# A list scheduler that models a port shared by VectorE and GpSimd, with new costs, and an opening whose products all run on VectorE

## The chip, the cores and the metric

The kernel runs on one core of one Trainium2 chip. The core has five engines, each with an instruction queue that is worked off in order: TensorE (PE, with its weight loads PEld), VectorE (DVE), ScalarE (ACT), GpSimd (POOL) and SyncE (SP), which here issues the DMA transfers. The metric is the device time of one execution in microseconds (us). Of the kernel before there are three timed runs and one profiled execution.

## The reference

Two layers of a trunk, on 512 latent tokens and a prefix of 256 context tokens, with 1024 channels. In each layer both streams are scaled and shifted by vectors that depend on `c` and `c_ctx`, projected by one wide weight `w_in`, sent through three branches, merged by sigmoid gates, projected back, and normalised with the residual. Cut to what matters:

```python
def trunk_layer(x, ctx, c, c_ctx, p, ang_r, ang_c, need_ctx):
    shift, scale, gate = jnp.split(jax.nn.silu(c) @ p['w_ada'] + p['b_ada'], 3, axis=-1)
    shift_c, scale_c, gate_c = jnp.split(jax.nn.silu(c_ctx) @ p['w_ada'] + p['b_ada'], 3, axis=-1)
    h = x * (1.0 + scale[:, None, :]) + shift[:, None, :]
    hc = ctx * (1.0 + scale_c) + shift_c
    ... = jnp.split(h @ p['w_in'], pts, axis=-1)
    ... = jnp.split(hc @ p['w_in'], pts, axis=-1)
    ...
    y_attn = blocked_attention(ql, k_all, v_all) * jax.nn.silu(a_g)
    ...
    y_gla = gla_finish(ol_f + flip(ol_b), p['gla_o_norm'], x.dtype) * jax.nn.silu(g_g)
    y_sgu = sgu(s_u, s_v, ...) * jax.nn.silu(s_g)
    ...
    m = (jax.nn.sigmoid(ga) * (ya @ p['w_br_attn']) + jax.nn.sigmoid(gg) * (yg @ p['w_br_gla'])
         + jax.nn.sigmoid(gs) * (ys @ p['w_br_sgu']))
    out = m @ p['w_out']
    x_new = layer_norm(DEEPNORM_ALPHA * x + gate[:, None, :] * out, p['post_g'], p['post_b'])
```

The context stream takes the same way in layer 0; in layer 1 only its keys, values and states are needed. "GLA" is a gated linear attention in chunks, in both directions; "SGU" a gated MLP that mixes positions within 128 tokens.

## The kernel before

**Arithmetic.** Each operand of a large product is held as a pair of a high and a low part in a 32-bit type that PE multiplies quickly; `mm3` makes one product with three matmuls (high × high, high × low, low × high). Names that end in h or l are such pairs: `wh`/`wl` and `hi`/`lo` of weights, `hlh`/`hll` of the latent rows, `hch`/`hcl` of the context rows. `split(hi, lo, src)` makes a pair: ACT copies `src` into `hi`, then `lo = src - hi` is a subtraction with two operands in SBUF. `wgroup` does that for 128 rows of a weight at a time: SP loads `raw`, then comes a split.

**Pieces of either engine.** `tta` records an elementwise operation of two tensors as `sc.alt`: either DVE or POOL may do it, and the scheduler decides which (profile line L126). All `lo`, `wl`, `hll` and `hcl`, the multiplications by rotary tables, most of the GLA's decay products `M`, the rows `P` of the softmax and parts of the last norm are such pieces. Instructions of one fixed engine go through `call` (profile line L395).

**What sets the order.** The class `Sched` records every instruction with its engine (or engines), what it reads and writes, a cost in ns from `_cost`, and a place in program order, shifted by biases per stage. `order` then works through a model of the five engines: on each the instruction that is first in priority among those that are ready is put next. An alternative piece stands in the ready lists of both engines, and the one that comes to it first has it. Before the change the engines of this model are independent but for data, buffer places and DMA. `issue` repeats this for 12 rounds, with priorities mixed from the last round's times, keeps the order with the shortest modelled end, and writes it out. So each engine's queue is fixed at build time, and costs alone can move any instruction.

**The opening.** `start0` makes the shift and scale of layer 0 and the projections of q, k and v for 8 blocks of 128 channels, `kb`. For each, `load` brings blocks of `w_ada`, and `dots(kb, v, npool)` multiplies them by rows of silu(c) (stream v = 0, latent) or silu(c_ctx) (v = 1, context), four products of 128x512 each, summed along the row. On DVE product and sum are one `scalar_tensor_tensor`; on POOL the product is a `tensor_tensor` and ACT makes the sum. `NPOOL` says how many of the four POOL takes for v = 1: 2 in each block, 16 in all. Two small sums give `svec`, the shift and scale; `modulate` applies them to `xs` (on ACT or DVE) and splits the result into hlh/hll or hch/hcl; the rows of `w_in` are split into wh/wl; and `mmt` multiplies. A block of `w_ada` keeps its place until the products of both streams are done.

Of the kernel before, what the change touches and what calls it, by code (L numbers as in the profile page):

```python
# [20 lines left out]
EPS = 1e-6  # L21
# [6 lines left out]
class Sched:  # L28
    """Records the kernel's instructions in program order, with what each reads and writes, and issues
    them in the order a list scheduler finds: on each engine the first in priority of those that are  # L30
    ready. Tiles of one tag take their places in program order."""
# [5 lines left out]
    def __init__(self, nc):  # L37
        self.nc = nc
        self.ops = []
        self.tiles = {}  # L40
        self.tags = {}
        self.state = {}
        self.masks = {}
        self.bias = 0.0
        self.floor = -1e9
        self.label = "start"
        for n, e in (("PE", nc.tensor), ("ACT", nc.scalar), ("DVE", nc.vector), ("POOL", nc.gpsimd), ("SP", nc.sync)):
            setattr(self, n, _Eng(self, n, e))
# [40 lines left out]
    def record(self, eng, fn, outs, ins, cost, table=None, dens=0.0):  # L89
        i = len(self.ops)  # L90
        deps, names, raw = set(), set(), set()
        rd = [r for r in map(self.region, ins) if r]
        wr = [r for r in map(self.region, outs) if r]
        for name, q, m in rd:
            names.add(name)
            W, R = self.state.setdefault(name, ([], []))
            psum = self.tiles[name][3] == "PS"
            raw.update(j for j, q2, m2 in W if q & q2 and m & m2)
            if psum:
                deps.update(j for j, q2, m2 in R if q & q2 and m & m2)  # L100
        for name, q, m in wr:
            names.add(name)
            W, R = self.state.setdefault(name, ([], []))
            deps.update(j for j, q2, m2 in W + R if q & q2 and m & m2)
            W[:] = [x for x in W if x[1] & ~q or x[2] & ~m]
            R[:] = [x for x in R if x[1] & ~q or x[2] & ~m]
            W.append((i, q, m))
        for name, q, m in rd:
            self.state[name][1].append((i, q, m))
        deps |= raw  # L110
        deps.discard(i)
        self.ops.append((eng, fn, deps, names, cost, table, max(i + self.bias, self.floor), self.label, dens, raw))
        return i

    def group(self, eng, calls, outs, ins, cost, dens):
        """instructions of one engine that stay together"""
        return self.record(eng.n, lambda: [getattr(eng.e, m)(*a, **k) for m, a, k in calls], outs, ins, cost, None, dens)

    def alt(self, *ways):
        """one piece of work that each of several engines could do: ways are (engine, method, arguments)"""  # L120
        fns, costs = {}, {}
# [6 lines left out]
        return self.record(tuple(fns), fns, outs, ins, costs)  # L128
# [6 lines left out]
    def order(self, prio):  # L135
# [32 lines left out]
        recent, dense = collections.deque(), 0.0  # L168
        seq, when = [], [0.0] * n
# [3 lines left out]
        hold = [[] for _ in range(n)]  # L173
        ends = [0.0] * n
# [9 lines left out]
        def can(i):  # L184
            """a place for each tile the instruction is first to touch, or the tag to wait for"""
# [25 lines left out]
        while done < n:  # L211
# [33 lines left out]
            elif e == "PE" and len(R) > 1:  # L245
# [7 lines left out]
                else:  # L253
                    i = heapq.heappop(R)[1]
            else:
                i = heapq.heappop(R)[1]
            if gone[i]:
                continue
            k = can(i)
# [14 lines left out]
            st = t  # L274
            if e == "ACT" and ops[i][5] not in (None, cur):
                st = max(st, acted + 1283.0)
                cur = ops[i][5]
# [28 lines left out]
            else:  # L306
                end = free[e] = st + cost
                if e == "ACT":
                    acted = end
            when[i] = st  # L310
# [28 lines left out]
        # how late each could start with this order of the engines  # L339
# [15 lines left out]
    SWITCH = 100.0  # L355
    ROUNDS, MIX, ADJ = 12, 0.35, ("PE",)
# [20 lines left out]
class _Eng:  # L377
# [3 lines left out]
    def __getattr__(self, meth):  # L381
# [3 lines left out]
        def call(*a, **k):  # L385
# [9 lines left out]
            return s.record(n, lambda: real(*a, **k), outs, ins, _cost(n, meth, outs, ins, k), _table(n, k), _dens(n, ins, k))  # L395
# [4 lines left out]
def _dens(n, ins, k):  # L400
# [3 lines left out]
    return 0.7 * d if "tile_position" in k else d  # L404

# [6 lines left out]
def _cost(n, meth, outs, ins, k):  # L412
# [4 lines left out]
    if n == "PE":  # L417
        if meth == "transpose":
            return 56.0 if ins[0].dtype == F32R else 109.0
# [3 lines left out]
        if ins[0].dtype == F32R:  # L423
            return max(sz / 2.4 + 2.5, 0.84 * m)
        if "tile_position" in k:
            return 21.0 + 0.4 * sz
        return max(4 * sz / 2.4, 1.68 * m) + 4
# [3 lines left out]
    if n == "DVE":  # L431
        psum = any(str(x.space).endswith("PSUM") for x in ins + outs)
        if meth == "reciprocal":
# [8 lines left out]
    if n == "POOL":  # L442
        if k.get("op") == ALU.pow:
            return 165.0 * sz + 300
        if meth == "tensor_tensor":
            return 2.08 * sz + 115
# [4 lines left out]
        return 3.4 * sz + 150  # L451
# [7 lines left out]
def kernel(ctx: ExitStack, tc: tile.TileContext, A, out, dbg=None):  # L459
# [87 lines left out]
    AH, NPOOL, NP0 = 2, (2, 2), 0  # L547
# [6 lines left out]
    def wgroup(src, nkb, c0, n, tags=None, scale=None):  # L554
        """hi/lo parts of the weight columns c0..c0+n, one pair of k-blocks each"""
# [22 lines left out]
    def mm3(ps, L, R, first, last):  # L578
        """ps += L^T R with both operands as (hi, lo) pairs"""
# [4 lines left out]
    def cm(wt, o, m, X, seg, tag="p"):  # L584
        """channel-major block: out[m channels, tokens of seg]"""
# [8 lines left out]
    def tm(wt, o, n, X, t, tag="p"):  # L594
        """token-major block: out[tokens of tile t, n columns]"""
# [14 lines left out]
    def ada_rows(nv, tag=None):  # L610
        """silu(c) and silu(c_ctx) along the free axis of all partitions"""
# [17 lines left out]
    def ada_dot(l, blk, sv, sums):  # L629
        """one channel block (128) of silu([c, c_ctx]) @ w_ada, in halves of the sum"""  # L630
# [12 lines left out]
    def ada_gate(l, nv, sums, gd):  # L643
        """the gate's rows into DRAM, from sums [channel, stream, block, half]"""
# [19 lines left out]
    def layer(l, X, start=None):  # L664
# [8 lines left out]
        def qs_(seg):  # L673
            """columns of a tensor over the query tokens"""
# [43 lines left out]
        def norm_q(t):  # L718
# [4 lines left out]
            rsqrt_(ss[:, 0:8], ss[:, 0:8], 8, 1.0, 64 * EPS)  # with the scores' 1/8  # L723
# [140 lines left out]
        def scores(t, g, pr):  # L864
            """softmax rows of two heads"""
# [78 lines left out]
        # decays: c[.., j] = sum of the chunk's first j log decays (times 16)  # L944
# [32 lines left out]
        for pr in range(2):  # L977
# [5 lines left out]
            # keys carried to the chunk's ends, both directions stacked on the partitions  # L983
# [30 lines left out]
            # queries carried from the chunk's start  # L1014
# [10 lines left out]
            # inside the chunk: pairs whose nearest common block has 2^lv tokens, seen from its middle  # L1025
            ng = n_o // 2
            for gi in range(2):
# [4 lines left out]
                for lvs in LEVELS:  # L1032
                    ps = PS("s", [128, 2, 512])
                    calls, kq, views, off, cost = [], [], {}, 0, SWITCH_PE
                    for lv in lvs:
# [8 lines left out]
                        if lv == 1:  # L1044
                            # a key lies at its pair's middle: the keys as they are, the queries as they are and carried
# [197 lines left out]
        # last branch: its sigmoids first, so that h's place can take the merged rows  # L1243
# [125 lines left out]
    X0 = new_h(0)  # L1369

    def start0():
# [9 lines left out]
        def mmt(t, k, o, ps, joint=False):  # L1381
            """joint: a block of a bank that is zeroed as a whole"""
# [22 lines left out]
        def dots(kb, v, npool):  # L1405
            """shift and scale of the channel block kb for one stream"""
# [86 lines left out]
def _layout(inp):  # L1493
# [15 lines left out]
    # small parameters side by side  # L1509
# [8 lines left out]
    # constants of the shapes alone  # L1518
# [32 lines left out]
```

## Time and profile before

| | us |
|---|---|
| three runs | 1522.32, 1522.93, 1525.35 |
| median | 1522.93 |
| span of the profiled execution | 1524.9 |

The profile page gives, of that one execution, each engine's busy time with its share and its instructions, slices of the span, the chain of work that ended last, and groups of instructions by line. The trace answers closer questions: windows (busy time of each engine in a stretch, with the clock that PE was granted), the timeline of one engine, groups kept apart by shape. A line reads: line of the kernel, engine, operation, output <- inputs, their shape, count, then busy us and the mean in ns, and in brackets or behind a bar how long the engine stood before and what released it. "Busy" counts an instruction from start to end, also where it stands for a port. The stages lie as follows: the opening up to about 85 us, attention of layer 0 with projections for the GLA to 305, GLA of layer 0 to 490, further projections ("fill"), merge and output to 925, attention of layer 1 to 1095, its GLA to 1245, fill and merge to 1443, and the tail of output product and norm.

### The profile page before, as it was taken

To read this page: it belongs to the slowest core of one execution; us is meant where nothing else is said; L and a number is where in the kernel's file an instruction comes from. 1 tells how busy PE (TensorE), PEld (TensorE's weight loads), DVE (VectorE), ACT (ScalarE), POOL (GpSimd) and SP (SyncE) were. 2 spreads that over 40 slices of the span, in tenths; PEclk is the share of its full clock that TensorE was granted. 3 is DMA by queue.
4 is the path that set the end of the run, shared out by engine and by line. 5 is a ranking of instruction groups with operands and counts; after the bars stand their busy time and mean duration, and the time that the engine had idled before them with its cause. 6 is when DMAs were issued, how large, how long until landed. Compare 5 with 4: busy or idle time off the path is not lost.

```text
span 1524.9 us, 27418 instructions
## 1 busy us (share of the span) xinstructions
PE 1420.7 (93%) x10724; PEld 1244.6 (82%) x10724; DVE 1071.1 (70%) x1928; ACT 660.5 (43%) x1288; POOL 577.8 (38%) x546
## 2 busy tenths in 40 slices
PE   7799999978998999999999999899978989999977
PEld 5698899867787888888889999888956778888867
DVE  8968887897868778432166765787798794443496
ACT  4466666734452222322231365566644442422321
POOL 5534332477665222110031253333367651100275
PEclk9999999989999999999999999999979999999999
DMA  7410111311265455222232232012322365333342
GB/s 270 158 54 12 29 29 56 121 50 55 84 204 170 153 159 154 86 67 62 64 101 94 97 97 60 8 29 70 113 69 77 117 222 153 98 96 104 97 138 90
DMA packets 115891, 151.23 MB, mean 99 GB/s; under 512 B 8601, under 2 KB 89905, under 8 KB 115761
## 3 DMA queue, kind: packets, MB, share of 16 engines
q1 hardware_dynamic: 115762, 149.49, 31.4%
q8 instruction: 84, 1.38, 0.4%
q14 instruction: 45, 0.37, 0.1%
HBM read 134.76 MB, written 14.69 MB: 98 GB/s over the span
## 4 chain that ended last, share of the span: by engine, by line
PE 50%; DVE 13%; POOL 3%; issue 3%; ACT 1%; DMA 1%; POOLq 0%; SPq 0%; ACTq 0%; DVEq 0%
PE p L395 45%; PE pt L395 3%; DVE lo L126 2%; PE s L395 2%; DVE M L126 1%; DVE rA L126 1%; POOL M L126 1%; DVE sm L395 1%; DVE sv L126 1%; POOL sf L395 1%; DVE sgS L395 1%; DVE cs L395 0%; DVE PTs L395 0%; DVE raw L126 0%; DVE mac L126 0%
## 5 line engine op out<-in xcount | busy, mean ns | idle before, releaser
L126 DVE TENSOR_TENSOR lo<-raw,hi 128x512 fp32r<-128x512 f32 (+1 forms) x204 | 170.1, 841 | 227.6 <-ACT hi L395 224.1
L126 POOL TENSOR_TENSOR lo<-raw,hi 128x512 fp32r<-128x512 f32 (+1 forms) x92 | 132.5, 1443 | 462.2 <-ACT hi L395 372.9
L395 PE MATMUL p<-hlh,lo 128*128 128x512 f32 x704 | 283.7, 403 | 7.0 <-DVE lo L126 6.9
L395 PE MATMUL p<-hlh,hi 128*128 128x512 f32 x704 | 284.1, 403 | 4.2 <-ACT keep L126 2.2
L395 ACT ACTIVATE hi<-raw 128x512 fp32r<-128x512 f32 (+1 forms) x296 | 185.1, 633 | 234.1 <-PE p L395 160.8
L395 PE MATMUL p<-hll,hi 128*128 128x512 f32 x704 | 282.8, 402 | 0.0
L395 PEld LDWEIGHTS p<-hlh,lo 128*128 128x128 f32 x704 | 134.5, 191 | 39.3 <-DVE lo L126 9.0
L395 PEld LDWEIGHTS p<-hlh,hi 128*128 128x128 f32 x704 | 134.2, 191 | 31.4 <-ACT keep L126 2.7
L395 PEld LDWEIGHTS p<-hll,hi 128*128 128x128 f32 x704 | 134.3, 191 | 27.4
L395 PE MATMUL p<-hch,hi 128*128 128x256 f32 x368 | 105.1, 285 | 0.0
L395 PE MATMUL p<-hch,lo 128*128 128x256 f32 x368 | 105.0, 285 | 0.0
L395 PE MATMUL p<-hcl,hi 128*128 128x256 f32 x368 | 104.9, 285 | 0.0
L395 PE MATMUL p<-lo,hlh 128*128 128x256 f32 (+1 forms) x352 | 101.0, 287 | 1.1 <-DVE lo L126 0.8
L395 PE MATMUL p<-hi,hlh 128*128 128x256 f32 (+1 forms) x352 | 101.9, 289 | 0.0
L395 PE MATMUL p<-hi,hll 128*128 128x256 f32 (+1 forms) x352 | 101.0, 287 | 0.0
L395 ACT ACTIVATE sig<-p 128x512 f32<-128x512 f32 (+1 forms) x48 | 25.3, 526 | 130.0 <-PE p L395 129.5
L395 DVE TENSOR_REDUCE sm<-s 128x1 f32<-128x768 f32 (+1 forms) x72 | 65.0, 921 | 17.5 <-PE s L395 17.1
L395 ACT ACTIVATE P<-s,sm 128x768 f32<-128x768 f32 (+1 forms) x80 | 65.1, 819 | 19.7 <-DVE sm L395 19.5
L395 DVE TENSOR_TENSOR PTs<-pt,PTs 128x512 fp32r<-128x512 f32 x104 | 69.4, 683 | 4.7 <-ACT PTs L395 3.5
L395 PEld LDWEIGHTS p<-hch,hi 128*128 128x128 f32 x368 | 70.3, 191 | 2.1
L395 PEld LDWEIGHTS p<-hcl,hi 128*128 128x128 f32 x368 | 70.2, 191 | 1.9
L395 PE MATMUL pt<-PTs,V 128*128 128x256 f32 x416 | 64.6, 289 | 7.2 <-DVE PTs L395 7.1
(327 smaller groups left out, 3761.7 us busy)
## 6 DMA issues: line engine op xcount, KB each, us to landing
raw<-in_w_in_dram SPq DMA_DIRECT2D x204, 256.0 KB, 2.9
wada<-in_w_adaT_dram SPq DMA_DIRECT2D x80, 256.0 KB, 5.1
raw<-in_w_out_dram SPq DMA_DIRECT2D x32, 256.0 KB, 2.7
raw<-in_w_in_dram SPq DMA_DIRECT2D x16, 272.0 KB, 2.9
wada<-in_w_adaT_dram SPq DMA_DIRECT2D x8, 512.0 KB, 5.4
raw<-in_w_br_attn_dram SPq DMA_DIRECT2D x16, 256.0 KB, 3.0
raw<-in_w_br_gla_dram SPq DMA_DIRECT2D x16, 256.0 KB, 3.0
raw<-in_w_br_sgu_dram SPq DMA_DIRECT2D x16, 256.0 KB, 2.9
```

The source lines that it names most:

```text
L126: fns[p.n] = lambda real=real, k=k: real(**k)
L395: return s.record(n, lambda: real(*a, **k), outs, ins, _cost(n, meth, outs, ins, k), _table(n, k), _dens(n, ins, k))
```

## The change

A list of ports stands beside the recorded instructions. `_port` names who holds the shared port: every POOL instruction that reads SBUF, and on DVE those with two or more inputs in SBUF, as well as copies and operations with scalars where neither side is in PSUM:

```diff
+def _port(n, meth, outs, ins):
+
+    inside = [x for x in ins if x.space == bass.MemoryType.SB and any(c > 1 for _, c in x.ap[1:])]
+    if n == "POOL":
+        return (n,) if any(x.space == bass.MemoryType.SB for x in ins) else ()
+    if n == "DVE":
+        psum = any(x.space == PSUM for x in list(ins) + list(outs))
+        if len(inside) > 1 or meth in ("tensor_copy", "tensor_scalar") and not psum:
+            return (n,)
+    return ()
```

In `order` such an instruction starts no earlier than the other engine's hold ends. While the other engine holds the port, the choice among the ready instructions adds that wait, times `HOLD`, to the priority of those that need the port. And POOL leaves an alternative piece for later if DVE, with what stands ahead of the piece in its ready list, would still be done with it sooner than POOL:

```diff
+            elif e in held and R and held[other[e]] > t + 1.0:
+
+                w = held[other[e]] - t
+                c = min(R, key=lambda x: x[0] + (self.HOLD * w if e in self.port[x[1]] else 0.0))
+                R.remove(c)
+                heapq.heapify(R)
+                i = c[1]
             else:
                 i = heapq.heappop(R)[1]
             if gone[i]:
                 continue
+            if e == "POOL" and isinstance(ops[i][4], dict) and len(ops[i][4]) > 1 and i not in put:
+
+                back = max(0.0, free["DVE"] - t) + sum(ops[j][4]["DVE"] if isinstance(ops[j][4], dict) else ops[j][4] for p_, j in ready["DVE"] if not gone[j] and p_ < prio[i])
+                if back + ops[i][4]["DVE"] < self.LEAVE * ops[i][4]["POOL"]:
+                    heapq.heappush(later["POOL"], (t + max(back, 100.0) + ops[i][4]["DVE"], i))
+                    continue
...
             st = t
+            if e in held and e in self.port[i]:
+                st = max(st, held[other[e]])
...
+                if e in held and e in self.port[i]:
+                    held[e] = end
...
+    HOLD, LEAVE = 1.0, 1.0
```

The costs (ns; `sz` is the free size) and the opening's constant:

```diff
-            return 56.0 if ins[0].dtype == F32R else 109.0
+            return 62.0 if ins[0].dtype == F32R else 110.0
...
-            return max(sz / 2.4 + 2.5, 0.84 * m)
+            return max(0.4475 * sz + 2.5, 0.84 * m)
...
-        return max(4 * sz / 2.4, 1.68 * m) + 4
+        return max(1.73 * sz, 1.68 * m) + 2
...
+        if meth == "tensor_tensor_scan":
+            return 2 * sz / 0.96 + 50
+        if len(outs) > 1:
+            return (sz + 64) / 0.96 + 40
...
-            return 2.08 * sz + 115
+            few = any(st == 0 and c > 1 for x in ins for st, c in x.ap[1:])
+            return (1.7 if few else 2.2) * sz + 125
...
-        return 3.4 * sz + 150
+        return 0.9 * sz + (135 if meth == "tensor_copy" else 175)
...
-    AH, NPOOL, NP0 = 2, (2, 2), 0
+    AH, NPOOL, NP0 = 2, (0, 0), 0
```

Comments and docstrings are dropped as well. The arithmetic of the kernel is the same. The changed kernel has 1820 DVE instructions where there were 1768, 472 on POOL where there were 546, and 1177 on ACT where there were 1171; PE and SP have as many as before.

What that does to the queues, first POOL's in the opening. Before, from its eleventh row on (`wada` is a product of `dots`, `rope` a preparation of the rotary tables, lo of 128x544 a weight split for the GLA's projections):

```order
L395 TENSOR_TENSOR wada<-wada,srow 128x512 x4
L126 TENSOR_TENSOR wl<-raw_113,wh 128x768
L395 TENSOR_TENSOR wada<-wada,srow 128x512 x2
L126 TENSOR_TENSOR wl<-raw_117,wh 128x768
L126 TENSOR_TENSOR hcl<-xs,hch 128x256
L126 TENSOR_TENSOR hll<-xs,hlh 128x512
L395 TENSOR_TENSOR wada<-wada,srow 128x512 x2
L126 TENSOR_TENSOR hcl<-xs,hch 128x256
```

And POOL's queue now, from the same place (L128 is the line of `alt` after the change):

```order
L128 TENSOR_TENSOR hll<-xs,hlh 128x512
L128 TENSOR_TENSOR hcl<-xs,hch 128x256
L128 TENSOR_TENSOR wl<-raw_139,wh 128x768
L128 TENSOR_TENSOR rope_142<-rope_141,pkl 128x256
L128 TENSOR_TENSOR hcl<-xs,hch 128x256
L128 TENSOR_TENSOR rope_143<-rope_141,pkl 128x256 x2
L128 TENSOR_TENSOR rope_142<-rope_141,pkl 128x256
L128 TENSOR_TENSOR lo<-raw,hi 128x544 x2
L128 TENSOR_TENSOR hcl<-xs,hch 128x256
L128 TENSOR_TENSOR lo<-raw,hi 128x544 x2
L128 TENSOR_TENSOR hcl<-xs,hch 128x256
```

The 16 products are gone to DVE, one hll and one wl stay where there were three and four, and rotary and weight work of the next stage now stands between the context's hcl.

DVE's queue at the end of the opening, before (`a2s` and `V` belong to the next stage):

```order
L126 TENSOR_TENSOR wl<-raw_139,wh 128x768
L395 TENSOR_TENSOR svec_73<-aa 128x2
L395 TENSOR_TENSOR svec_73<-svec_73,pk 128x2
L126 TENSOR_SCALAR xs<-xs,svec_73 128x256
L126 TENSOR_TENSOR lo<-raw,hi 128x544
L126 TENSOR_TENSOR hcl<-xs,hch 128x256
L126 TENSOR_TENSOR rope_143<-rope_141,pkl 128x256 x2
L126 TENSOR_TENSOR rope_142<-rope_141,pkl 128x256
L395 TENSOR_TENSOR a2s<-a2r,a2s 64x512
```

And now, from the last hll of the latent stream on:

```order
L128 TENSOR_TENSOR hll<-xs,hlh 128x512
L419 SCALAR_TENSOR_TENSOR wada,aa<-wada,srow 128x512 x3
L419 TENSOR_TENSOR svec_73<-aa 128x2
L419 SCALAR_TENSOR_TENSOR wada,aa<-wada,srow 128x512
L419 TENSOR_TENSOR svec_73<-svec_73,pk 128x2
L419 SCALAR_TENSOR_TENSOR wada,aa<-wada,srow 128x512 x2
L419 TENSOR_TENSOR a2s<-a2r,a2s 64x512
L419 TENSOR_REDUCE sm<-ksq 128x4
L419 TENSOR_TENSOR svec_73<-aa 128x2
L419 TENSOR_TENSOR V<-s,V 128x2x64
L419 TENSOR_TENSOR svec_73<-svec_73,pk 128x2
```

The last products of the context stream stand behind all latent splits, and a2s and the first V have moved ahead of the last hcl.

POOL at the start of layer 0's GLA, before (`M<-cs` are subtractions that build decays, `M<-M,qk` the products with q or k, `lo` a weight split of the fill):

```order
L126 TENSOR_TENSOR Eq<-cs 128x768
L126 TENSOR_TENSOR qx<-qk,Eq 64x768
L126 TENSOR_TENSOR M<-cs 128x192 x2
L126 TENSOR_TENSOR M<-cs 128x96x2 x2
L126 TENSOR_TENSOR M<-cs 128x48x4
L126 TENSOR_TENSOR qx<-qk,Eq 64x768
L126 TENSOR_TENSOR M<-M,qk 128x768
L126 TENSOR_TENSOR lo<-raw,hi 128x512
L126 TENSOR_TENSOR qx<-qk,Eq 64x768
L126 TENSOR_TENSOR M<-cs 128x24x8
L126 TENSOR_TENSOR M<-M,qk 128x768
```

And now:

```order
L128 TENSOR_TENSOR Eq<-cs 128x768
L128 TENSOR_TENSOR qx<-qk,Eq 64x768
L128 TENSOR_TENSOR M<-cs 128x192 x2
L128 TENSOR_TENSOR M<-cs 128x96x2 x2
L128 TENSOR_TENSOR M<-cs 128x48x4 x2
L128 TENSOR_TENSOR M<-M,qk 128x384
L128 TENSOR_TENSOR M<-cs 128x48x4
L128 TENSOR_TENSOR M<-cs 128x24x8
L128 TENSOR_TENSOR lo<-raw,hi 128x512
L128 TENSOR_TENSOR M<-cs 128x24x8 x2
L128 TENSOR_TENSOR M<-M,qk 128x768
L128 TENSOR_TENSOR M<-cs 128x12x16 x3
```

POOL has more of the subtractions and fewer of the wide products. Over the stage, in layer 0 it makes 70 of the subtractions where it made 51, and 3 of the products of width 768 where it made 10; in layer 1 it has 74 and 4 where it had 52 and 11. Of the softmax rows P it makes 6 and 5 pieces where it made 10 and 13, of the weight splits lo of 128x512 it makes 31 where it made 92, and of the fill's 6 and 6 where it made 11 and 14.

More of the change, by code (lines that the diff above doesn't have):

```diff
@@ L39, in __init__ @@
         self.ops = []
+        self.port = []
         self.tiles = {}
@@ L87, in region, with record @@
         return name, q, m
-    def record(self, eng, fn, outs, ins, cost, table=None, dens=0.0):
+    def record(self, eng, fn, outs, ins, cost, table=None, dens=0.0, port=()):
         i = len(self.ops)
@@ L112, in record @@
         self.ops.append((eng, fn, deps, names, cost, table, max(i + self.bias, self.floor), self.label, dens, raw))
+        self.port.append(port)
         return i
@@ L119, in alt @@
     def alt(self, *ways):
-        fns, costs = {}, {}
+        fns, costs, port = {}, {}, []
         for p, meth, k in ways:
@@ L127, in alt @@
             costs[p.n] = _cost(p.n, meth, outs, ins, k)
-        return self.record(tuple(fns), fns, outs, ins, costs)
+            port += _port(p.n, meth, outs, ins)
+        return self.record(tuple(fns), fns, outs, ins, costs, port=tuple(port))
     def lag(self, a, b, raw=False):
@@ L168, in order @@
         recent, dense = collections.deque(), 0.0
+        held = {"DVE": 0.0, "POOL": 0.0}
+        other = {"DVE": "POOL", "POOL": "DVE"}
         seq, when = [], [0.0] * n
@@ L173, in order @@
         hold = [[] for _ in range(n)]
+        put = ()
         ends = [0.0] * n
@@ L394, in call @@
             ins = aps + [v for q, v in k.items() if isinstance(v, bass.AP) and q not in ("out", "accum_out")]
-            return s.record(n, lambda: real(*a, **k), outs, ins, _cost(n, meth, outs, ins, k), _table(n, k), _dens(n, ins, k))
+            return s.record(n, lambda: real(*a, **k), outs, ins, _cost(n, meth, outs, ins, k), _table(n, k), _dens(n, ins, k), _port(n, meth, outs, ins))
         return call
```

## The prediction

> **What bounds the kernel now.** I read the head of the page first: the span and the busy line.
>
> ```profile
> span 1524.9 us, 27418 instructions
> PE 1420.7 (93%) x10724; PEld 1244.6 (82%) x10724; DVE 1071.1 (70%) x1928; ACT 660.5 (43%) x1288; POOL 577.8 (38%) x546
> ```
>
> PE is busy for 93% of the span, and the matmuls are the same 10724 after the change as before. Only time in which PE stands, or runs slowly spaced, can be won. Which stages have such time is read from the view of windows, cut at the program's stages (columns: window, length, busy us and count of PE, PEld, DVE, ACT, POOL, the granted clock, DMA share, GB/s).
>
> ```profile
> 10.00:85.00 75.00, 58.66 (x268) 46.43 (x268) 73.69 (x143) 35.12 (x75) 46.28 (x30) 0.91 0.55 191
> 85.00:305.00 220.00, 213.39 (x1568) 199.04 (x1567) 174.34 (x340) 148.37 (x327) 75.91 (x73) 1.00 0.17 50
> 305.00:490.00 185.00, 162.54 (x2201) 139.28 (x2200) 155.65 (x256) 78.28 (x136) 125.47 (x125) 0.96 0.33 106
> 490.00:860.00 370.00, 369.77 (x2259) 329.42 (x2258) 205.03 (x397) 96.85 (x174) 68.73 (x50) 1.00 0.34 106
> 925.00:1095.00 170.00, 161.00 (x1165) 149.51 (x1165) 129.33 (x233) 105.06 (x215) 55.91 (x49) 0.99 0.17 49
> 1095.00:1245.00 150.00, 124.35 (x1444) 97.91 (x1443) 133.87 (x252) 74.07 (x137) 101.83 (x126) 0.93 0.38 116
> 1245.00:1443.00 198.00, 198.00 (x858) 160.55 (x857) 86.94 (x134) 65.45 (x110) 23.15 (x18) 1.00 0.40 117
> 1443.00:1500.00 57.00, 46.76 (x306) 42.33 (x305) 51.63 (x55) 14.16 (x23) 40.54 (x22) 0.94 0.37 120
> ```
>
> In 490–860 and 1245–1443 (fill, merge, output products) PE is busy for 369.77 of 370 and 198.00 of 198 us: nothing that the change does to DVE or POOL there is worth anything. PE stands 16.3 us in the opening (75 − 58.66), 6.6 and 9.0 in the two attentions (85–305, 925–1095), 22.5 and 25.7 in the two GLA stages, 10.2 in the tail. In the opening, the GLA stages and the tail DVE and POOL together are busy for more time than the window has: 73.69 + 46.28 in 75, 133.87 + 101.83 in 150. That looks like two engines working side by side; the timeline says otherwise.
>
> ```profile
> 20.26 2.33 POOL L126 TENSOR_TENSOR wl<-raw,wh 128x768 fp32r<-128x768 f32 x1
> 20.85 1.75 DVE L395 TENSOR_TENSOR svec<-aa 128x2 f32<-128x2 f32 x1
> ```
>
> A sum of two elements takes 1.75 us where it starts behind a POOL piece and ends with it (20.85 + 1.75 = 22.60; 20.26 + 2.33 = 22.59); by itself it takes 0.15 us, as a row further down shows. So a DVE operation with two SBUF inputs and a POOL operation that reads SBUF take turns, and much of "busy" is standing. This is the one resource that the change models, and it is what I price: the **sum** of both engines' undisturbed durations.
>
> The Trainium skill, "SBUF — State Buffer", section "SBUF: two separate sides", calls the pair of ports that these engines share "an exclusive lock, not a bandwidth split". The 1.75 us agree. If the two shared bandwidth instead, POOL's removed products would free nothing and DVE's added ones would lengthen the opening; the sums below go by the rows alone.
>
> **The change, part by part.** *The opening.* It moves 16 products of 128x512 from POOL (with an ACT accumulation each) to DVE, and with them the planner moves splits: the subtractions wl go from 4 on DVE and 4 on POOL to 7 and 1, hll from 5 and 3 to 7 and 1, hcl stays at 4 and 4. Undisturbed durations:
>
> ```profile
> 6.10 0.69 DVE L395 SCALAR_TENSOR_TENSOR junk<-wada,srow 128x512 f32<-128x512 f32 x1 [4.37 <-ACT srow L395]
> ...
> 24.05 1.38 POOL L395 TENSOR_TENSOR wada<-wada,srow 128x512 f32<-128x512 f32 x1 [1.46 <-DVE junk L395]
> ...
> 29.36 1.84 POOL L126 TENSOR_TENSOR wl<-raw,wh 128x768 fp32r<-128x768 f32 x1
> ...
> 31.75 0.68 DVE L395 SCALAR_TENSOR_TENSOR wada<-wada,srow 128x512 f32<-128x512 f32 x1
> ...
> 32.37 0.68 DVE L395 SCALAR_TENSOR_TENSOR wada<-wada,srow 128x512 f32<-128x512 f32 x1
> ...
> 47.02 0.15 DVE L395 TENSOR_TENSOR svec<-aa 128x2 f32<-128x2 f32 x1
> 47.09 0.95 DVE L126 TENSOR_TENSOR wl<-raw,wh 128x768 fp32r<-128x768 f32 x1
> ...
> 77.88 1.28 POOL L126 TENSOR_TENSOR hll<-xs,hlh 128x512 fp32r<-128x512 f32 x1 [1.41 <-ACT hlh L395]
> 79.12 1.35 POOL L126 TENSOR_TENSOR lo<-raw,hi 128x544 fp32r<-128x544 f32 x1
> 80.44 0.73 POOL L126 TENSOR_TENSOR rope<-rope,pkl 128x256 f32<-128x256 f32 x1
> ...
> 81.88 0.41 DVE L126 TENSOR_TENSOR hcl<-xs,hch 128x256 fp32r<-128x256 f32 x1
> ...
> 83.99 0.28 PE L395 MATMUL pt<-wh,hcl 128*128 128x256 f32 x1
> ```
>
> Recorded DVE times overlap the next by 0.06 to 0.07 us (31.75 + 0.68 against 32.37; 47.02 + 0.15 against 47.09), so the steps are 0.62 for a product, the same for hll (an estimate by the equal shape), 0.88 for wl, 0.34 for hcl, 0.07 for one of 32 small sums. Before, DVE: 48 × 0.62 + 4 × 0.88 + 5 × 0.62 + 4 × 0.34 + 32 × 0.07 = 40.0 us. POOL: 16 × 1.38 + 4 × 1.84 + 3 × 1.28 + 4 × 0.73 = 36.2 us (hcl by the rope row of equal shape). Taken in turns that is 76.2 us, and from the first product at 6.10 to the last split's end (81.88 + 0.41 = 82.29) the trace has 76.2. The opening is bound by this turn-taking and by nothing else; PE's matmuls with that split follow, at 83.99 one of the last.
>
> After, DVE: 64 × 0.62 + 7 × 0.88 + 7 × 0.62 + 4 × 0.34 + 32 × 0.07 = 53.8. POOL's queue up to its last hcl, by the order, holds one hll, one wl, four hcl, and of later work four rope pieces and four lo of 128x544: 1.28 + 1.84 + 8 × 0.73 + 4 × 1.35 = 14.4. Sum 68.2, or 8.0 less. DVE's queue also has pieces ahead of its last hcl that stood behind it (the copy-sum a2s, sums for q and k, V): I count some 2 us for them, an estimate by three 128x512-wide steps; V waits for PE there, so the last hcl may stand later without PE standing. **Taken: −6**, bounds 0 (something else, such as ACT's hlh or the weights' places, is as late as the port was) and −8. The 16 accumulations leave ACT, which has 35.12 of 75 busy and doesn't bind. SP issues the same transfers; the places of wada go free when the second stream's products are done, which is no later than before if the sum shrinks.
>
> *Later stages.* Only how pieces of either engine are placed, and in what order, changes. Groups by shape (busy us, mean ns, idle before):
>
> ```profile
> L126 DVE TENSOR_TENSOR lo<-raw,hi 128x512 fp32r<-128x512 f32 x190 | 158.0, 838 | 217.2 <-ACT hi L395 213.8 <-PE p L395 2.2
> L126 POOL TENSOR_TENSOR lo<-raw,hi 128x512 fp32r<-128x512 f32 x90 | 129.7, 1444 | 460.9 <-ACT hi L395 371.7 <-PE p L395 89.0
> L126 DVE TENSOR_TENSOR M<-M,qk 128x768 f32<-128x768 f32 x14 | 16.7, 1189 | 1.1 <-ACT M L395 1.0
> L126 POOL TENSOR_TENSOR M<-M,qk 128x768 f32<-128x768 f32 x10 | 18.7, 1872 | 12.2 <-ACT M L395 12.1
> L126 DVE TENSOR_TENSOR M<-cs 128x192 f32<-128x192 f32 x53 | 26.0, 544 | 1.2 <-PE s L395 1.1
> L126 POOL TENSOR_TENSOR M<-cs 128x192 f32<-128x192 f32 x51 | 34.4, 701 | 10.0 <-issue 4.9 <-DVE qx L126 2.6 <-PE s L117 2.3
> L126 POOL TENSOR_TENSOR P<-P,sm 128x768 f32<-128x768 f32 x23 | 36.4, 1590 | 78.5 <-DVE sm L395 54.3 <-PE p L395 23.9
> L126 DVE TENSOR_SCALAR P<-P,sm 128x768 f32<-128x768 f32 x41 | 31.5, 768 | 1.2
> ```
>
> A piece moved from POOL to DVE frees 0.61 us of the port for a lo, 0.68 for a product M of 768, 0.82 for a P; a subtraction into M of 192 moved the other way costs 0.16. GLA of layer 0: 7 products go to DVE (−4.8), 19 subtractions to POOL (+3.0), and 5 lo of the fill to DVE (−3.0). The first two are on PE's path (M feeds the scores), the lo mostly lie behind PE's other work: **−2**, bounds −4.8 and +3.0. Layer 1 has pieces of two thirds the width, so 7 × 0.45 = −3.2 and 22 × 0.10 = +2.3, and 8 lo, −4.9: **−2.5**, bounds −5.8 and +2.3. Attention: 4 and 8 P pieces go to DVE, −3.3 and −6.6; POOL stood 78.5 us ahead of its 23, so they were late by their inputs, not by the port, and PE stands only 6.6 and 9.0 there: **−2.5** for both, bounds 0 and −9.9. Tail: two lo, **−1**, bounds 0 and −2; the gate's two products go to POOL, two pieces of the last norm come back, which I let cancel. Elsewhere 48 or so more lo move to DVE in stages where PE is the bound: 0. The new costs of PE, scan and the like change only the planned order; a gain from it is a rival below.
>
> Sum: −6 − 2 − 2.5 − 2.5 − 1 = −14, so a span of 1510.9. The three runs have a median of 1522.93, which is 2.0 under the profiled span; so **1509**.
>
> **Rivals.** *(1) The order gains too.* The planner now takes the turns into account, so that DVE or POOL picks work that needs no turn while the other works. If that took away a third of the 48.2 us that PE stands in the two GLA stages, 16 us more: 1493. For it: DVE is busy or blocked there for 155.65 of 185 and 133.87 of 150 us. Against it: nearly every alternative of either engine there reads two SBUF inputs, so there is little to choose.
>
> *(2) It doesn't convert.* The opening's end is set by the next thing at once, and elsewhere PE's other work hides the rest: 1518 to 1526, middle 1522. For it: 93% busy on PE, and POOL's ten M products of 768 stood 12.2 us for ACT. Against: the opening's sum closes to 0.1 us with the trace. The Trainium skill, "Perfetto Trace Analysis", section "Optimizing Scalar/DVE Operations", warns that because of the shared port offloading between these two "might not help"; that speaks for this rival where a piece takes as long on both, but the rows have 1.38 against 0.62.
>
> *(3) Slower: DVE inherits POOL's waits.* DVE works in order. Before, POOL waited for ACT's high half (1.41 us ahead of the hll at 77.88) and DVE went on. After, DVE does 7 hll and 4 hcl itself, with products and sums queued behind each, and the next k-block's shift and scale wait for those, then ACT, then PE. At 1.41 us each that is 15.5 us; less the 6 won, +9.5 in the opening, and with the later gains half there 1529. It decides from 6 / 11 = 0.55 us a split (opening's gain gone) and 14 / 11 = 1.3 us (all gone). Against it: before, DVE did 5 hll and 4 hcl and was busy for 73.69 of 75 us, hardly ever waiting.
>
> **How the numbers follow.** Forecast 0.54 (own range 1501 to 1518), rival 1 0.14, rival 2 0.16, rival 3 0.16. Below 1495 lies over half of rival 1, above 1527 most of rival 3, together 0.2: the range is 1495 to 1527. About 0.2% (3 us) is what a measurement of this kernel can tell from no change: faster takes the forecast, rival 1 and a quarter of rival 2, 0.72; the rest of rival 2, 0.12, is the same; slower 0.16.
>
> **What would show it.** In the changed profile the last hcl of the opening ends near 76 us (at most 80, where V stands ahead of it) and PE's last matmuls with it near 78; no svec sum there takes over 1 us except beside the ten or so POOL pieces. If DVE shows idle time before hll or hcl of over 0.5 us each, rival 3 is at work. PE's standing time in the GLA stages falls by 2 to 3 us each; by 8 each, it is rival 1. In 490–860's counterpart nothing changes. I am wrong if the opening is as long as before although POOL's share of it fell by half, or if the GLA stages grow by more than the opening wins.

## The result, and the profile after

The changed kernel takes 1490.7 us (median of 4 runs, 1488.61 to 1491.66) where the kernel before took 1523.47 beside it: a ratio of 0.9783, with a 95% interval from 0.9767 to 0.9799. That is 33 us faster. The forecast was 14 us faster (1509, range 1495 to 1527): right in its direction, too small by more than half, and the time lies below the range. The head of the page after, its span and busy line:

```profile
span 1488.3 us, 27349 instructions
PE 1409.4 (95%) x10724; PEld 1246.0 (84%) x10724; DVE 1039.7 (70%) x1996; ACT 672.9 (45%) x1286; POOL 435.9 (29%) x472
```

DVE does 68 instructions more than before in 31 us less of "busy", so what went there is not work but standing at the port. An estimate of how much: at the median time that each shape takes on DVE in the run all_dve below, where POOL has none of the either-engine pieces, DVE's instructions would take 957 us before and 1018 after; their recorded times, which overlap a little, add up to 1157 and 1137. So some 200 us of waiting became 120. The 142 us that POOL loses are mostly work that moved away: 61 splits `lo` at 1.44 us and 16 products at 1.38 are 110 us by themselves. The windows of the kernel after, with the bounds moved to where the same stages now lie (columns as before):

```profile
10.00:72.00 62.00, 52.97 (x258) 44.40 (x258) 61.05 (x164) 29.74 (x50) 19.10 (x14) 0.92 0.69 235
72.00:288.00 216.00, 211.28 (x1557) 197.14 (x1556) 173.41 (x342) 148.40 (x327) 66.29 (x60) 1.00 0.17 46
288.00:473.00 185.00, 165.63 (x2240) 145.47 (x2239) 153.23 (x252) 81.74 (x139) 124.44 (x141) 0.95 0.36 117
473.00:842.00 369.00, 366.99 (x2238) 327.05 (x2237) 198.24 (x433) 95.94 (x173) 15.98 (x15) 1.00 0.34 103
904.00:1059.00 155.00, 151.38 (x1103) 140.62 (x1103) 125.82 (x239) 105.09 (x216) 38.26 (x36) 1.00 0.15 44
1059.00:1218.00 159.00, 142.38 (x1576) 117.29 (x1574) 131.98 (x247) 91.78 (x160) 102.01 (x137) 0.95 0.46 138
1218.00:1408.00 190.00, 184.54 (x786) 149.46 (x787) 84.35 (x138) 62.13 (x103) 5.16 (x4) 0.97 0.38 107
1408.00:1464.00 56.00, 48.32 (x306) 44.12 (x305) 51.97 (x59) 14.25 (x23) 30.99 (x18) 0.91 0.38 124
```

In the opening PE stands 9 us where it stood 16.3. The window of the first GLA is as long as it was (185 us), with 19 us of standing instead of 22.5. In the second, PE stands 16.6 of 159 us instead of 25.7 of 150: the window is longer, but holds 132 PE instructions more, which before lay in other stages. So stages can't be compared by their length alone.

To have one measure for all kernels here, PE's work is counted in us: each matmul by the spacing that its shape has where matmuls follow each other densely in the trace of before (the lower quartile of its start-to-start times). That makes 1315 us for every kernel. The time that has passed when PE has done so much of it, less that work, is PE's lost time. By pieces of the work, up to the last matmul, from the traces of the runs described below (the first 50 us are the opening, 250 to 450 and the end of 800 to 1100 hold the GLA, 50 to 250 and the start of 800 to 1100 the attention, 450 to 800 and 1100 to 1250 the stages that PE bounds):

```
PE's lost time, us    0-50   50-250  250-450  450-800  800-1100  1100-1250  1250-end   sum
before                32.5    17.5     53.7      9.2      71.3        1.1       15.5   200.8
after                 20.3    16.7     48.3      6.8      57.6        1.1       14.1   165.0
npool_only            31.4    18.6     55.6     12.2      66.5        1.1       16.5   202.0
costs_only            33.8    39.0     49.8     14.1      77.1        1.1       20.4   235.3
newassign_oldplan     24.0    18.0     59.7     12.4      54.2        1.1       16.4   185.9
oldassign_newplan     29.5    14.3     57.6      5.0      71.0        1.1       18.0   196.6
leave0                30.6    14.0     54.7      5.5      73.2        1.1       13.7   192.9
leave_only            31.5    27.0     54.0      6.4      70.9        1.1       13.7   204.7
port_oldcost          21.9    15.0     70.2      5.9      72.8        1.1       14.9   201.9
pe_oldcost            26.8    12.4     62.7      6.2      72.5        1.1       13.2   195.0
pool_oldcost          29.7     13.6     57.6      7.0      60.4        1.1       11.8   181.2
port_npool22          35.1    17.6     46.7      6.0      56.1        1.1       11.3   174.0
all_dve_oldplan       15.6    12.1     57.1      4.4      67.4        1.1        6.1   163.8
all_dve_noport        14.6     12.9     55.4      4.5      55.9        1.1        5.2   149.8
all_dve               15.2    13.7     50.5      4.5      57.7        1.1        6.0   148.7
leave3                19.4    18.4     42.9      5.4      51.9        1.1        8.4   147.6
```

The gain of the change, 35.8 us by this measure, is 12.2 in the opening, 13.7 in layer 1's attention and GLA, 5.4 in layer 0's GLA, and 4.6 elsewhere. (The spans of the two profiled executions are 36.6 us apart, the medians of the timed runs 33.) The measure counts slowly spaced matmuls with the standing. Matmuls that start while the clock granted to PE is at half make 20.9 us of the lost time before and 17.9 after, and the mean granted clock is 0.978 and 0.975, so the gain doesn't come from the clock.

### The profile page after: what moved, and what is told of

Read it like the earlier page. It is cut to its first block, busy times and chain, and to the rows that moved or that the text cites. A ratio compares the mean times of both kernels' runs of the same rounds, so it can differ in the third digit from the quotient of the medians.

```text
span 1488.3 us, 27349 instructions
## 1 busy us (share of the span) xinstructions
PE 1409.4 (95%) x10724; PEld 1246.0 (84%) x10724; DVE 1039.7 (70%) x1996; ACT 672.9 (45%) x1286; POOL 435.9 (29%) x472
## 3 DMA queue, kind: packets, MB, share of 16 engines
q8 instruction: 84, 1.38, 0.4%
## 4 chain that ended last, share of the span: by engine, by line
PE 79%; DVE 8%; ACT 4%; POOL 3%; DMA 3%; issue 2%; SPq 0%; POOLq 0%; ACTq 0%; DVEq 0%
PE p L419 64%; PE pt L419 9%; PE s L419 5%; PE s L119 2%; DVE sm L419 1%; ACT L419 1%; DVE lo L128 1%; DMA wada<-in_w_adaT_dram 1%; ACT ez L419 1%; DVE junk L419 1%; POOL ymix L128 1%; DVE wada L419 1%; DMA raw<-in_w_in_dram 1%; DVE PTs L419 1%; DMA sgc<-in_sgu_ln_g_dram 1%
## 5 line engine op out<-in xcount | busy, mean ns | idle before, releaser
L128 DVE TENSOR_TENSOR lo<-raw,hi 128x512 fp32r<-128x512 f32 (+1 forms) x265 | 202.8, 771 | 227.4 <-ACT hi L419 218.8
L128 POOL TENSOR_TENSOR M<-cs 128x192 f32<-128x192 f32 (+1 forms) x144 | 82.0, 598 | 17.7 <-DVE cs L419 5.7
L128 POOL TENSOR_TENSOR raw<-raw,gate 128x512 f32<-128x512 f32 x10 | 16.8, 1682 | 201.0 <-DMA raw<-in_w_out_dram 200.9
L419 DVE SCALAR_TENSOR_TENSOR wada<-wada,srow 128x512 f32<-128x512 f32 x96 | 69.7, 734 | 5.4 <-DMA wada<-in_w_adaT_dram 4.0
```

Source lines behind the costliest of these rows:

```text
L128: fns[p.n] = lambda real=real, k=k: real(**k)
```

## The experiments

Times are medians beside runs of the kernel before on the same chip (1524 to 1525 us there); all were timed in three rounds or more.

**One part alone: the constant.**

```diff
 (kernel before)
-    AH, NPOOL, NP0 = 2, (2, 2), 0
+    AH, NPOOL, NP0 = 2, (0, 0), 0
```

> The kernel before with NPOOL (0, 0) alone: old planner, old costs, all 64 products of the opening on DVE. Before is 1523.5 us, the whole change 1490.7. If the constant alone makes the opening's part of the gain (PE loses 12.2 us less there in the changed trace), 1511. If the opening gains only because the planner then knows the port and puts the context's products behind the latent splits, 1518 to 1524.

Measured 1528.6, ratio 1.0025 (1.0008 to 1.0041): a little slower. The opening loses 31.4 us in place of 32.5. The old planner fills POOL's time again: it gives POOL 19 of the opening's either-engine pieces, where it gave 12 before beside the 16 products, and the changed planner gives 10.

**The other way round: all but the constant.**

```diff
 (changed kernel)
-    AH, NPOOL, NP0 = 2, (0, 0), 0
+    AH, NPOOL, NP0 = 2, (2, 2), 0
```

> The changed kernel with NPOOL (2, 2) as before: 16 products of the opening back on POOL, all else as changed. By the sum of undisturbed durations the opening is then 12 us longer (POOL 22 more, DVE 10 less): 1500 to 1504. If the constant is worth only what npool_only shows in the opening (1 us), 1490 to 1494.

Measured 1500.3, 0.9845 (0.9823 to 0.9868). With the new planner the constant is worth 9.6 us, and the opening's lost time is 35.1 against 20.3. So it paid only with the planner that doesn't refill POOL.

**Costs, port, leaving: which of them?** costs_only takes the port out of the plan's times and sets LEAVE to 0; leave0 keeps the port and sets LEAVE to 0; leave_only takes out the port alone; port_oldcost undoes all of the diff's lines in `_cost`. The diff of costs_only, of which leave0 is the last pair of lines and leave_only the others:

```diff
 (changed kernel)
-            if e in held and e in self.port[i]:
-                st = max(st, held[other[e]])
...
-                if e in held and e in self.port[i]:
-                    held[e] = end
...
-    HOLD, LEAVE = 1.0, 1.0
+    HOLD, LEAVE = 1.0, 0.0
```

> The changed kernel without the port model (no instruction waits for a port in the plan, POOL leaves nothing): new costs and NPOOL (0, 0). If the refitted costs bring the later stages' gain (20 us beyond the opening in the trace), near 1491 to 1497. If the port model brings it, near the time of npool_only, 1508 to 1520.

> The changed kernel with LEAVE 0: the plan knows the port and chooses by it, but POOL takes any ready piece of either engine as before (493 such pieces on POOL where the changed kernel has 328). If POOL's leaving is what brings the gain, near npool_only or slower, 1520 to 1560. If the modelled port (order) is, 1491 to 1500.

> The changed kernel without the port in the plan's times, but POOL still leaves a piece that DVE would finish sooner (274 pieces on POOL). If fewer pieces on POOL are the cause, close to the changed kernel or better, 1485 to 1500. If leaving only helps where the plan knows the waits, 1505 to 1525.

> The changed kernel with the costs of before (port model, leaving, NPOOL (0, 0) kept; 359 pieces on POOL). If the refitted spacings matter, 1503 to 1520; if the port model and the leaving carry the gain by themselves, 1489 to 1498.

```
costs  port  leaving   us        ratio (95%)
old    no    no        1528.6    1.0025 (1.0008 to 1.0041)   npool_only
new    no    no        1559.2    1.0236 (1.0213 to 1.0259)   costs_only
new    yes   no        1520.9    0.9978 (0.9965 to 0.9992)   leave0
new    no    yes       1529.3    1.0038 (1.0020 to 1.0055)   leave_only
old    yes   yes       1526.5    1.0017 (1.0001 to 1.0032)   port_oldcost
new    yes   yes       1490.7    0.9783 (0.9767 to 0.9799)   the change
```

Whichever of the three is left out, at most 8 of the 38 us against npool_only are left. npool_only, costs_only, leave_only and port_oldcost came out slower than any answer that their expectations offered. New costs by themselves cost 31 us, and in the presence of the other two they are worth 36. A single "which part did it" has no answer; the later runs ask what the parts act on.

**Which engine, or which order?** Each of the 1016 either-engine pieces is fixed to one engine, and only the order is left to the planner. newassign_oldplan is npool_only with the changed kernel's engines, oldassign_newplan the changed kernel with npool_only's.

```diff
     def alt(self, *ways):
...
+        if any(w[0].n == "POOL" for w in ways):
+            fix = _FIXED[self.alts]
+            ways = [w for w in ways if w[0].n[0] == fix]
+            self.alts += 1
```

> npool_only with every piece that DVE or POOL may do fixed to the engine that the changed kernel gives it (387 of 1016 pieces differ from npool_only's own choice); order by the old planner with old costs. If the gain beyond the opening is the sum of shorter pieces on DVE, as my forecast had it, most of the changed kernel's time is reached: 1491 to 1498. If it is the order, near npool_only, 1506 to 1515.

> The changed planner and costs, with every such piece fixed to the engine that npool_only gives it. If the gain beyond the opening is from the engines chosen, near npool_only, 1506 to 1515. If it is from the order, which knows the turns at the port, 1491 to 1498.

Measured 1511.6, 0.9929 (0.9906 to 0.9952), and 1522.0, 0.9988 (0.9972 to 1.0005). Against npool_only's 1528.6 the engines alone bring 17 us, the order alone 6.6, both 37.9. Both answers that the expectations offered were too simple: the engines are the larger part, but more than a third of the gain needs engines and order together.

**Is it luck of the order?** One lag in the plan is changed by 1 ns.

```diff
-    SAME = {"DVE": 127.0, "ACT": 148.0, "POOL": 96.0}
+    SAME = {"DVE": 128.0, "ACT": 148.0, "POOL": 96.0}
```

> The changed kernel with one number of its plan changed by 1 ns (the lag of DVE after itself, 127 to 128), which nobody would expect to matter, but which gives another order. If the gain comes from what the plan now knows, within 6 us of the changed kernel's 1490.7. If it is one lucky order among many, 1497 to 1520.

Measured 1486.9, 0.9763 (0.9745 to 0.9781), 4 us better than the change. One such kernel can't give the spread of all, but the gain doesn't hang on one order.

**Which cost?** The changed kernel with the old costs of one engine each; for PE:

```diff
 (changed kernel)
-            return 62.0 if ins[0].dtype == F32R else 110.0
+            return 56.0 if ins[0].dtype == F32R else 109.0
...
-            return max(0.4475 * sz + 2.5, 0.84 * m)
+            return max(sz / 2.4 + 2.5, 0.84 * m)
...
-        return max(1.73 * sz, 1.68 * m) + 2
+        return max(4 * sz / 2.4, 1.68 * m) + 4
```

For POOL the lines of `tensor_tensor` and of the last return, for DVE those of the scan and of two outputs, are put back as the diff of the change has them.

> The changed kernel with PE's costs as before (matmul spacing sz/2.4 + 2.5 in place of 0.4475 sz + 2.5, so PE has some 7% less to do in the plan); port, leaving and the other costs as changed. All old costs gave 1526.5. If PE's spacing is the refit that matters, 1510 to 1527; if not, 1489 to 1496.

> The changed kernel with POOL's costs as before (a subtraction with a repeated input no cheaper than a product of two full ones, other operations dearer). If POOL's refit decides which pieces it gets in the GLA, 1505 to 1527, with the loss in the two GLA stages; if not, 1489 to 1496.

> The changed kernel with DVE's costs as before (the scan of the decays at half its length, nothing added for a second output, as in the opening's products). If the scan is what the plan lacked, 1500 to 1527, with the loss in the GLA stages or the opening; if not, 1489 to 1496.

Measured 1519.1, 0.9976 (0.9960 to 0.9992), for PE; 1506.9, 0.9897 (0.9874 to 0.9920), for POOL; 1494.7, 0.9810 (0.9793 to 0.9828), for DVE. PE's costs, in the main 7% of spacing, are the refit that matters most: 28 us, 14 and 15 of them in the two pieces of work with the GLA. The last output of the fill's matmuls, which PE has to put between the GLA's steps, suggests why. With PE's old spacing it comes 35 us ahead of the first GLA's last output (414.9 against 450.1), so PE has nothing left to put there and loses 44 us over the 25 us of work at the GLA's end. In the changed kernel it comes 2.6 us ahead (425.7 against 428.3), and that loss is 25 us. In the kernel before the fill outlasts the GLA (458.3 against 440.4) and only 3.9 us are lost there; what it loses lies earlier in the GLA. No run moved the fill alone, so this account is not shown by itself. POOL's refit is worth 16 us, 9.4 of them in the opening and 9.3 in layer 0's GLA, less 2.4 elsewhere. DVE's 4 us are about what a change of 1 ns moved.

**Can the turns be taken away altogether?** leave3 sets LEAVE to 3, so that POOL leaves nearly everything but the GLA's subtractions `M<-cs` (152 pieces on POOL, 115 of them these; 328 pieces in the changed kernel). all_dve fixes all 1016 to DVE in the changed kernel.

```diff
 (changed kernel, leave3)
-    HOLD, LEAVE = 1.0, 1.0
+    HOLD, LEAVE = 1.0, 3.0
```

```diff
 (changed kernel with alt as in newassign_oldplan, all_dve; the string holds 1016 times D, cut here)
+_FIXED = "".join("""DDDDDDDDDDDD...
```

> The changed kernel with LEAVE 3: POOL leaves a piece unless DVE would need over three times as long to get it done. If fewer pieces on POOL are better as long as DVE has time, 1475 to 1488, faster than the changed kernel. If LEAVE 1 is already where the two balance, 1488 to 1500.

> The changed planner, costs and constant, with every one of the 1016 pieces that DVE or POOL may do fixed to DVE (328 of them are POOL's in the changed kernel). My forecast's reasoning, that a piece costs the port less on DVE, says each moved piece gains: 1475 to 1488. The rival, that POOL's help is still needed where DVE works on PSUM and leaves the port free, in the GLA and in attention: 1495 to 1530.

Measured 1473.1, 0.9662 (0.9643 to 0.9681), and 1473.7, 0.9661 (0.9645 to 0.9677), both just below the lower ends that the expectations gave: 17 us faster than the changed kernel, and 52 than the kernel before beside them. The page of all_dve, its span and busy line, and three of its groups by shape (busy us, mean ns, idle before), the last with its counterpart of before (L395):

```profile
span 1472.0 us, 27227 instructions
PE 1402.4 (95%) x10724; PEld 1235.5 (84%) x10724; DVE 1054.1 (72%) x2326; ACT 672.3 (46%) x1284; POOL 85.8 (6%) x144
```

```profile
L145 DVE TENSOR_TENSOR M<-cs 128x192 f32<-128x192 f32 x104 | 31.4, 368 | 1.6 <-PE s L436 1.4
L145 DVE TENSOR_TENSOR lo<-raw,hi 128x512 fp32r<-128x512 f32 x280 | 190.7, 689 | 208.6 <-ACT hi L436 202.8 <-PE p L436 3.9
L436 DVE TENSOR_TENSOR svec<-aa 128x2 f32<-128x2 f32 x16 | 2.4, 157 | 0.0
L395 DVE TENSOR_TENSOR svec<-aa 128x2 f32<-128x2 f32 x16 | 13.3, 830 | 0.6 <-ACT wada L395 0.6
```

This is the plainest reading of the case. DVE does everything that POOL was helping with, 398 instructions more than before, and is busy for 17 us less than before (1054.1 against 1071.1). The same subtraction that is recorded with 544 ns on DVE before takes 368 ns when POOL has none of these pieces, the split `lo` 689 in place of 838, and the sums of two elements 157 in place of 830.

leave3 takes the same time by another way. Its 115 subtractions on POOL go with 13 us less of lost time in the pieces with the GLA than all_dve has (42.9 and 51.9 us against 50.5 and 57.7), and it loses 9 us more in the opening and the attention (19.4 and 18.4 against 15.2 and 13.7). So POOL's help may still pay in the GLA. A kernel with POOL in the GLA alone was not run.

**Turns and costs apart.** With hardly a turn to take, the plan is tried with old costs (all_dve_oldplan, the kernel before with NPOOL (0, 0)) and with new ones but no port (all_dve_noport).

> The kernel before with NPOOL (0, 0) and every such piece fixed to DVE: old planner, old costs, and hardly any turn to be taken at the port, so the plan lacks nothing but the new spacings. all_dve gave 1473.7. If the loss of before was that its plan didn't know the turns, then without turns the old plan is good too: 1475 to 1492. If the new costs are worth as much by themselves as in the changed kernel (36 us), 1505 to 1515.

> costs_only (1559.2) with every such piece fixed to DVE: new costs, no port in the plan. If costs_only was slow because its plan had POOL work where it blocks DVE, this is 1472 to 1478, as all_dve, and the port model has nothing left to do. If knowing the port matters for the few POOL instructions that stay (rsqrt, resets), 1480 to 1500.

Measured 1488.2, 0.9749 (0.9723 to 0.9774), and 1476.5, 0.9674 (0.9642 to 0.9706). So the old planner with its old costs, which knows nothing of the port, is as fast as the whole change once POOL is left out: that brings 40.4 us (1528.6 to 1488.2). It takes away both the turns and POOL's own longer times (1444 ns for a `lo` on POOL before, 689 on DVE in all_dve), and the runs don't tell the two apart. The pieces of work that gain are the opening (31.4 to 15.6 us lost against npool_only), the attention of layer 0 (18.6 to 12.1), the stages from 450 to 800 (12.2 to 4.4) and the end (16.5 to 6.1), not the GLA. The new costs are then worth 12 us, nearly all of it in layer 1's attention and GLA (67.4 to 55.9), and modelling the port another 3, which the measurements don't tell from nothing, since the intervals overlap. In costs_only's plan the new costs were harmful (1559) because of POOL's pieces: with the pieces on DVE the same planner takes 1476.5.

## Why the prediction was wrong

**What bounds the kernel: right.** PE bounds it, and turns at the port make DVE slow; the stages that PE fills gave little (1.1 us lost in 1100 to 1250 in every kernel, 9.2 and then 6.8 in 450 to 800).

**The opening, −6: the port sum held, the step from it to PE failed.** The prediction put the last hcl near 76 us and took its 6 us for the opening's gain. Timelines of the changed kernel (DVE, then POOL, then PE):

```profile
63.84 0.69 DVE L128 TENSOR_TENSOR hll<-xs,hlh 128x512 fp32r<-128x512 f32 x1 [0.23 <-ACT hlh L419]
...
65.06 1.85 DVE L419 SCALAR_TENSOR_TENSOR wada<-wada,srow 128x512 f32<-128x512 f32 x1
...
76.11 0.42 DVE L128 TENSOR_TENSOR hcl<-xs,hch 128x256 fp32r<-128x256 f32 x1
```

```profile
64.44 1.93 POOL L128 TENSOR_TENSOR lo<-raw,hi 128x544 fp32r<-128x544 f32 x1 [14.11 <-ACT hi L419]
```

```profile
76.30 0.29 PE L419 MATMUL p<-hi,hlh 128*128 128x272 f32 x1
...
78.39 0.40 PE L419 MATMUL pt<-wh,hcl 128*128 128x512 f32 x1
```

And PE's first matmul of the next stage before the change:

```profile
90.66 0.29 PE L395 MATMUL p<-hi,hlh 128*128 128x272 f32 x1
```

The last hcl ends at 76.53, 5.8 us earlier than before: the forecast's number. But PE reaches the next stage at 76.30, 14.4 us earlier, ahead of the first matmul that can read that hcl (78.39). Of the 14.4 us, 12.2 are time that PE no longer loses, and the rest are context matmuls that it now makes later. The last hll, for the latent rows, is done at 64.53 (79.16 before), because the context's last products now stand behind all of the latent's. Five of the next stage's weight splits, `lo` of 128x544, are done by 74.7 (86.6 before), and PE works on them while the context's last block is made. What the port released first mattered more than when it released the last piece. The other kernels agree. leave0's last hcl comes 5 us later than before (87.3), and it still loses less there than before (30.6 against 32.5 us). newassign_oldplan, port_oldcost and the changed kernel have their last hcl within 0.2 us (76.6, 76.4, 76.5), and lose 24.0, 21.9 and 20.3; the ends of PE's matmuls for the latent rows (74.8, 71.3, 69.7) go in that order. Over the sixteen kernels of the table, the lost time of the opening goes with the end of the last hll: 14.6 to 15.6 us where it ends at 60.5 to 61.4, 19.4 to 24.0 at 63.8 to 67.3, 26.8 to 35.1 at 71.7 to 81.8. No run moved the last hll alone. So the step that failed is the one from the port's last piece to PE, "PE's matmuls with that split follow", and the term measured 12.2 instead of 6.

**The GLA, −2 and −2.5, and the attention, −2.5: the reason itself was wrong for the GLA.** I priced moved pieces by their shorter time on DVE. The groups of the changed kernel:

```profile
L128 DVE TENSOR_TENSOR M<-M,qk 128x768 f32<-128x768 f32 x21 | 22.9, 1109 | 1.2 <-ACT M L419 1.0
L128 POOL TENSOR_TENSOR M<-M,qk 128x768 f32<-128x768 f32 x3 | 5.5, 1842 | 1.0 <-ACT M L419 1.0
L128 DVE TENSOR_TENSOR M<-cs 128x192 f32<-128x192 f32 x34 | 19.2, 598 | 0.6 <-PE s L419 0.4
L128 POOL TENSOR_TENSOR M<-cs 128x192 f32<-128x192 f32 x70 | 43.8, 655 | 10.8 <-DVE cs L419 5.7 <-PE pt L419 3.1 <-DVE qx L128 0.9
```

The pieces moved as foreseen (7 products one way, 19 subtractions the other), but the GLA didn't become shorter: from its first scan to its last product M it took 144.7 us before and takes 151.6 (layer 1: 121.1 and 134.1). What it won is that PE does more other work meanwhile: 101.5 us of work in that stretch before, 129.5 after (layer 1: 77.4 and 117.2). The step that failed is the sentence that the new costs "change only the planned order", which put them at nothing in the sum and left such a gain to rival 1, with a chance of 0.14. pe_oldcost shows them to be worth 14 and 15 us where the GLA is, and all_dve_oldplan that moving every piece to DVE, with old costs, leaves the lost time of the pieces with the GLA where it was (57.1 and 67.4 us, against 55.6 and 66.5 in npool_only). The prices per piece had waiting in them, too: they came from recorded means, such as 838 ns for a `lo` on DVE that takes 689 in all_dve. The term for layer 0's GLA measured 5.4 us instead of 2. In layer 1 the attention shares its 13.7 us with the GLA, since PE's work moves between them; how much each has was not settled, nor which pieces made the attention better. Layer 0's attention gave 0.8. So the terms for layer 1, 2.5 and a part of the attentions' 2.5, were the most undersized, and why the new order suits layer 1 so well stays open beyond the costs.

**The tail, −1, and the weight splits elsewhere, 0:** measured −1.4 and −2.4; the first about right, the second small.

**The rivals.** Rival 1, an order that knows the turns, named 1493, and the time came out there. Its mechanism is half of it: the new order with the old engines brought 6.6 us, and the rest came only with other engines for the pieces. Rival 2 is out. Rival 3, DVE inheriting POOL's waits for ACT, did not come: 0.23 us ahead of the last hll where POOL had waited 1.41, and in all_dve, where DVE does every split, the opening loses only 15.2 us. What the Trainium skill says in "Perfetto Trace Analysis", section "Optimizing Scalar/DVE Operations", that offloading between these engines "might not help", I had counted for rival 2. The runs agree with it, and for the planner of before they go further than I had used it: there the offloading cost 40 us. In leave3 the 152 pieces left on POOL cost nothing against all_dve.

## What to carry to other kernels

Where two engines take turns at a port, add up their undisturbed times before calling the second one help; if the first has room, the quickest trial is to give the second nothing (17 us better here than a planner that models the turns; leaving the second little but the GLA's subtractions was as good). When a stage is shortened, follow which product the next engine starts with, not which one comes last. A planner's costs are part of the kernel: 7% on PE's spacing was worth 28 us, and a better cost without the other parts of the model made things worse.

## What the runs showed of the hardware

Not expected was how much of two engines' busy time is standing. By the estimate above DVE waits some 200 us before and 120 in the changed kernel. With 328 pieces on POOL and 1016 − 328 on DVE the two are busy for 435.9 and 1039.7 us; with all on DVE, for 85.8 and 1054.1. POOL's 350 us bought DVE nothing: 328 pieces more fit into 14 us more of its busy time. In leave3, with 152 pieces on POOL, the two are busy for 199.3 and 1050.6 us.
